# Hybrid convolution and RG-LRU layer: the last pair of lru tiles alone forked, with a PSUM tile for each of its four sums, and the remainders of four lru weights made on VectorE

## The chip, the cores and the metric

The kernel runs on one core of a Trainium2 chip. The metric is the device time of one execution in microseconds; smaller is better. The kernel before took 732.24, 734.92 and 737.24 us in three runs, with the median 734.92.

## The reference

One layer works on a sequence of 1024 tokens of 1024 channels, in float32. The normalised and modulated input goes through a wide projection, whose columns feed two groups side by side: a convolution group (gated depthwise convolution of 31 taps, layer norm over channels, swish, and the pointwise product `pw2`) and a recurrence group (RG-LRU). Both results are joined and go through the output projection, whose result is scaled by a gate and added to the input.

```
u = h @ w_in[l]
cv, cg, cs, lx, ls = jnp.split(u, [...], axis=-1)
...
v = jax.nn.silu(layernorm(v, cln_g[l], cln_b[l]))
v = v @ pw2_w[l] + pw2_b[l]
y_conv = v * jax.nn.silu(cs)
...
y_lru = hs * jax.nn.silu(ls)
y = jnp.concatenate([y_conv, y_lru], axis=-1) @ w_out[l]
x = x + (1.0 + gate[:, None, :]) * y
return rmsnorm(x, final_g)
```

The part of `w_out` that meets `y_lru` is what the change touches. It is called the lru product here.

## The kernel before, in words

**Number format.** TensorE works in a reduced float32 format. To keep accuracy, every operand is split into a high part and a remainder (`yh` and `yl`, `whi` and `wlo`), and each product is three matmuls: high by high, high by low, low by high. A weight comes from DRAM into `raw`; ScalarE casts it to `whi`; the remainder is `raw - whi`. There are two ways to make a remainder. One is a subtraction on VectorE (or, early in the kernel, GpSimd). The other, `remainder` at L540, lets ScalarE write `-whi` into `wlo` and then adds the weight itself from DRAM by an accumulating transfer that GpSimd issues. For the lru weights, the tuple `LRV` names those that take the VectorE way; all others take the transfer. The lru weights 0 to 7 bear the numbers 40 to 47 in tile names, so `wlo41` is the remainder of lru weight 1.

**Stages.** The layer runs in this order: modulation and first products; 40 column tiles of the input projection with the convolution and recurrence interleaved; the lru product, 8 output tiles of 128 x 1024 in four pairs p = 0 to 3; the pointwise product `pw2` in four pairs; the rest of `w_out`; and the final norm. While TensorE works on the lru product, VectorE and ScalarE finish the convolution and do the layer norm: sums of `c` and `cr` (`csum`, `mean`), squares (`lnsq`, collected in `lnss`), the spread of the result by TensorE (`lnbc`), and the splitting of the normalised tiles into the operands of `pw2` (`vha`, `vla`, `vhb`, `vlb`, `vhc`, `vlc` and the like).

**A pair of the lru product** (`lru_pair`, L1405) has two output tiles, each in two halves of 512 columns, and the inner dimension in eight blocks of 128. On four of the blocks the two-by-two product of halves is made with seven quarter products instead of eight, named 1, y, 2, z, 3, s and 4, over sums of operands (`yhs`, `yls` for the data, `lsh` and `lsl` for the weights). The other four blocks are multiplied plainly.

A quarter product appears in more than one output, so its value has to be used at several places while it grows. Pairs that are not forked (p = 0 and 1 before) do it outside PSUM: after each step, `use` (L1607) takes the partial value out of PSUM, scales it by the gate and adds it to the SBUF tile `acc`; the first step of each half is a ScalarE evacuation, later ones are VectorE operations on 512 columns. They use two PSUM tiles of two banks, `lp` and `lx`, and one of a single bank, `ly`. Forked pairs (`FORKP`, p = 2 and 3 before) do it inside PSUM: ScalarE copies the value after quarter 1 from `lx` to `lp`, and the quarter y from `lx` to a SBUF buffer `lk`; VectorE writes `lx + lk` into the second half of `lp` after quarter 2, and into the second half of `lx` after quarter 3; TensorE goes on adding in all four halves. At the end each tile is evacuated once, 1024 wide. All four sums live in the two tiles `lp` and `lx`; the class `Bank` lets the planner treat the two halves of such a tile as separate.

**What sets the order.** All engines' instructions are put in order at build time by a planner that simulates the engines (`order`, L241). Among the operations that are ready it takes the one with the lowest priority number; priorities are position numbers of the stages plus small offsets, and the pair p has position n = 40 + 2p. `FORKN` is the offset of the copies and sums of a forked pair, `FEVN` that of its evacuations, and `LSN` says how far back the start is that releases the loads of `lsh` and `lsl` (1: the quarter 2 of the pair before, 2: its first plain product). The engines then run these fixed orders, waiting on semaphores where an operand or a buffer isn't ready. Buffers are limited: PSUM has three tiles of two banks ("mm": `ps`, `lp`, `lx`) and two of one bank ("acc": `ly`); `raw`, `whi` and `wlo` have two slots each (lru weights 5 to 7 have large buffers in their place); and 47 large SBUF buffers are shared by nearly everything else, so that for instance `vla` or `vlc` takes a buffer that an `acc` tile held, and waits until the store of that tile (`accd`, an accumulating transfer that GpSimd issues) is through. GpSimd's queue in this part holds these stores and the remainders by transfer; SP's queue holds the loads.

Of the kernel before, what the change touches and what calls it, by code (L numbers as in the profile page):

```python
# [16 lines left out]
T = 1024  # L17
# [87 lines left out]
FINP = -0.5  # L105
BCLATE = False
BEHIND = 0
FORKP = (2, 3)
FORKN = -1.0
FEVAC = ("ACT", "ACT")  # L110
FEVN = 0.3
QT = {(0, c): ("HW", "X") for c in "y234"}
PLACED = ("big",)
MARGINS = 2.0
LSN = 1
LWBS = (5, 6, 7)
LWG = 0
TERMS = {**{("pw2_0", c): ("HW", "X") for c in "1z"}, **{(f"out_{p}", "1"): ("HX", "W") for p in (0, 1, 2, 3)}, **{(f"pw2_{p}", "1"): ("HX", "W") for p in (1, 2, 3)}}
# [38 lines left out]
class Buf:  # L157
    def __init__(self, pool, name, dtype, parts):
        self.pool, self.name, self.dtype, self.parts = pool, name, dtype, parts
        self.left, self.tile = 0, None  # L160
        self.read, self.written = {}, {}
        self.banks = None

    def __call__(self):
        return self.tile


class Bank:
    def __init__(self):
        self.read, self.written = {}, {}  # L170


class Op:
# [4 lines left out]
class Plan:  # L178
# [23 lines left out]
    def op(self, eng, cost, emit, prio, r=(), w=(), table=None, after=(), reserve=0,  # L202
           columns=0, lock=False, lag=0.0, moved=0.0, flight=FLIGHT):
        o = Op()
        o.lag, o.moved, o.flight = lag, moved, flight
        o.eng, o.cost, o.emit, o.prio, o.table = eng, cost, emit, prio, table
        o.succ, o.ready, o.seq, o.reserve = [], 0.0, len(self.ops), reserve
        o.columns = columns
        o.lock = not lag and eng == "POOL" or eng == "DVE" and lock
        r, w = list(self.keys(r)), list(self.keys(w))  # L210
        preds = set(after)
        for k in r:
            if k in self.writer:
# [17 lines left out]
        o.psum = [(b, any(k[0] is b for k in w)) for b in o.bufs if b.pool in ("mm", "acc") and not b.banks]  # L231
        o.psum += [(k[0].banks[k[1]], k in w) for k in dict.fromkeys(r + w) if isinstance(k[0], Buf) and k[0].banks]
        self.ops.append(o)
        return o

# [145 lines left out]
def hymba_layer(ctx: ExitStack, tc: tile.TileContext, xT, vecs, mod_w, w_first, w_in,  # L381
# [224 lines left out]
    def half(b, i):  # L606
        return part(b, i * H, i * H + H)
# [797 lines left out]
    def lru_pair(p, n, use, firsts, tiles):  # L1405
# [50 lines left out]
                ops.setdefault(c, o)  # L1456

        if p in FORKP:
            x.banks, p0.banks = [Bank(), Bank()], [Bank(), Bank()]

            def plain(s, ps, h):
                for k in rest:
                    mm_k(n + g, ps, s, yh, yl, k, FULL[h:h + 1], first=-1)

            def both(h, to):
                TT(n + FORKN, "DVE", half(to, 1), half(x, 0), half(kept, 0), ALU.add, H, r=[(x, 0), kept],
                   w=[(to, 1)])

            def out_of(i, ps):
                m = 2 * p + i  # L1470
                if FEVAC[i] == "ACT":
                    ACT(n + FEVN + i, tiles[i], ps, AF.Copy, scale=gate1[:, m:m + 1], r=[ps, ("gate1", m)],
                        w=[tiles[i]])
                else:
                    TS(n + FEVN + i, tiles[i], ps, gate1[:, m:m + 1], None, ALU.mult, r=[ps, ("gate1", m)],
                       w=[tiles[i]], n=T)
# [12 lines left out]
            g = 0.4  # L1489
            quarter("3", "S3", "T3", x, 0, False)  # L1490
            both(0, x)
            g = 0.5
            quarter("s", "S4", "B22", p0, 1, False)
            plain(s0, p0, 1)
            out_of(0, p0)
            g = 0.6
            quarter("4", "A22", "T4", x, 0, False)
            plain(s1, x, 0)
            g = 0.7
            plain(s1, x, 1)  # L1500
            out_of(1, x)
            return ops["1"], ops["3"]
        for c in LORDERS.get(p, LORDER):
            g += 0.12
# [368 lines left out]
```

## Time and profile before

| | us |
|---|---|
| three runs | 732.24, 734.92, 737.24 |
| profiled execution | 731.9 |
| its span on the core | 730.1 |
| TensorE busy in the span | 717.0 |
| VectorE busy | 619.3 |
| ScalarE busy | 481.0 |
| GpSimd busy | 170.3 |
| mean granted TensorE clock | 0.997 |

In the rows of the profile, PE is TensorE's matmuls and PEld its weight loads, DVE is VectorE, ACT is ScalarE, POOL is GpSimd, and SP issues loads. A row of the timeline gives the start, the duration, engine, line, operation, output and inputs by the program's names (numbers left out), shape and count, and in brackets how long the engine had been idle before it and what ended the idle time. A row of the windows gives, for a stretch of the span, its length and each engine's busy time. "L580" is the plain product's matmul, "L1448" that of a quarter, "L756" those of `pw2` and `w_out`; "L452" is any two-operand operation of VectorE, "L444" its scale-and-add, "L425" a copy or cast and "L433" any other operation of ScalarE, and "L457" a transfer issued by GpSimd.

### The profile page before, as it was taken

The numbers are of one execution on the slowest core, as the hardware profiler recorded it, in microseconds if no ns is written. First come the engines' busy times: TensorE is split into PE (matmuls) and PEld (weight loads), VectorE is DVE, ScalarE is ACT, GpSimd is POOL, SyncE is SP. The second block draws the span as 40 slices with busy tenths as digits, with TensorE's granted clock in tenths as the row PEclk, the third lists the DMA queues.
The fourth block names the chain that finished last, engine by engine and source line by source line (L and its number), as shares of the span: only waits on it lengthen the run. The fifth ranks groups of instructions, "written<-read, shape, count | busy, mean of one in ns | idle before, by whom it ended". The sixth has DMA issues, their size and how long they took to land.

```text
span 730.1 us, 9057 instructions
## 1 busy us (share of the span) xinstructions
PE 717.0 (98%) x3268; PEld 595.6 (82%) x3268; DVE 619.3 (85%) x851; ACT 481.0 (66%) x618; POOL 170.3 (23%) x172
## 2 busy tenths in 40 slices
PE   9999999999999999999999999999899999999996
PEld 8888888888888888888888888878778888888885
DVE  7999999899699898798499994989498966999647
ACT  7650789566698866947949869827488635746322
POOL 0046334354443320233221120100101101110003
PEclk9999999999999999999999999999999999999998
DMA  8946349949989996799898895876935855775006
GB/s 339 406 172 174 58 119 246 262 101 214 216 196 238 243 231 183 169 236 210 176 226 233 226 179 151 256 191 187 223 58 110 228 139 131 232 187 185 30 14 217
DMA packets 46779, 138.58 MB, mean 190 GB/s; under 512 B 5280, under 2 KB 16544, under 8 KB 46624
## 3 DMA queue, kind: packets, MB, share of 16 engines
q0 software_dynamic: 20016, 53.40, 40.9%
q1 hardware_dynamic: 25712, 83.71, 32.7%
q10 hardware_dynamic: 1008, 0.92, 0.4%
q8 instruction: 25, 0.41, 0.2%
q14 instruction: 18, 0.15, 0.1%
HBM read 79.63 MB, written 22.54 MB: 140 GB/s over the span
## 4 chain that ended last, share of the span: by engine, by line
PE 85%; DVE 6%; ACT 4%; issue 3%; DMA 1%; DVEq 0%; POOLq 0%; ACTq 0%
PE ps L580 43%; PE xout L756 6%; PE xpw L756 6%; PE first L889 5%; PE lx L1448 3%; PE ypw L756 3%; PE lp L580 2%; PE lx L580 2%; PE gate L1309 2%; DVE caccs L444 2%; PE y L726 2%; PE zpw L756 2%; PE zout L756 1%; DMA wlo<-in_w_out_dram 1%; PE lp L1448 1%
## 5 line engine op out<-in xcount | busy, mean ns | idle before, releaser
L580 PE MATMUL ps<-uh,whi 128*128 128x512 f32 x576 | 177.5, 389 | 0.0
L580 PE MATMUL ps<-uh,wlo 128*128 128x512 f32 x576 | 177.3, 389 | 0.0
L580 PE MATMUL ps<-ul,whi 128*128 128x512 f32 x576 | 177.3, 389 | 0.0
L580 PEld LDWEIGHTS ps<-ul,whi 128*128 128x128 f32 x576 | 108.1, 188 | 22.5
L580 PEld LDWEIGHTS ps<-uh,wlo 128*128 128x128 f32 x576 | 108.1, 188 | 22.4
L580 PEld LDWEIGHTS ps<-uh,whi 128*128 128x128 f32 x576 | 108.0, 188 | 22.4
L457 POOL DMA_DIRECT2D es<-cq x45 | 40.2, 899 | 134.2 <-ACT cq L433 85.5
L425 ACT CAST whi<-raw 128x1024 fp32r<-128x1024 f32 (+1 forms) x44 | 44.9, 1026 | 37.4 <-issue 22.3
L452 POOL TENSOR_TENSOR wlo<-raw,whi 128x1024 fp32r<-128x1024 f32 x16 | 40.6, 2547 | 87.4 <-ACT whi L425 87.1
L433 ACT ACT_TABLE_LOAD x44 | 56.5, 1283 | 1.5 <-PEq L1865 0.7
L444 DVE SCALAR_TENSOR_TENSOR cacc<-v,V,cacc 128x511 f32<-128x511 f32 (+14 forms) x75 | 55.6, 741 | 0.4
L444 DVE SCALAR_TENSOR_TENSOR caccs<-v,V,caccs 128x511 f32<-128x511 f32 (+6 forms) x70 | 51.9, 742 | 2.0 <-ACT caccs L433 1.0
L444 DVE SCALAR_TENSOR_TENSOR caccs<-c,wsum,caccs 128x511 f32<-128x511 f32 (+6 forms) x70 | 52.0, 743 | 1.0
L457 POOL DMA_DIRECT2D oo<-co x39 | 37.2, 996 | 45.5 <-ACT co L433 20.4
L433 ACT ACTIVATE cq<-v,V 128x511 f32<-128x511 f32 (+14 forms) x45 | 31.8, 707 | 4.5 <-DVE modw L444 4.5
L452 DVE TENSOR_TENSOR wlo<-raw,whi 128x1024 fp32r<-128x1024 f32 (+1 forms) x23 | 27.4, 1194 | 8.4 <-ACT whi L425 8.4
L444 DVE SCALAR_TENSOR_TENSOR modw<-modw,sc 128x1024 f32<-128x1024 f32 x23 | 31.4, 1369 | 0.2 <-DMA modw<-in_mod_w_dram 0.2
L444 DVE SCALAR_TENSOR_TENSOR xs<-ps,V,xs 128x1023 f32<-128x1023 f32 (+2 forms) x24 | 30.6, 1273 | 0.5 <-ACT xs L433 0.5
L433 ACT ACTIVATE cq<-c,wsum 128x512 f32<-128x512 f32 x42 | 29.7, 711 | 0.0
L433 ACT ACTIVATE co<-v,V 128x510 f32<-128x510 f32 (+12 forms) x39 | 26.6, 706 | 0.0
L433 ACT ACTIVATE finsq<-fin 128x512 f32<-128x512 f32 (+2 forms) x14 | 7.9, 570 | 27.4 <-DVE fin L444 14.4
L452 POOL TENSOR_TENSOR o<-fin,bc 128x256 f32<-128x256 f32 (+1 forms) x8 | 7.8, 999 | 68.0 <-ACT bc L425 62.3
(409 smaller groups left out, 1591.4 us busy)
## 6 DMA issues: line engine op xcount, KB each, us to landing
raw<-in_w_in_dram SPq DMA_DIRECT2D x36, 512.0 KB, 5.8
modw<-in_mod_w_dram SPq DMA_DIRECT2D x24, 512.0 KB, 8.3
scsd<-scs SPq DMA_DIRECT2D x8, 512.0 KB, 4.3
raw<-in_w_out_dram SPq DMA_DIRECT2D x8, 512.0 KB, 3.8
accd<-acc POOLq DMA_DIRECT2D x8, 512.0 KB, 6.6
rawpw<-in_pw_dram SPq DMA_DIRECT2D x8, 512.0 KB, 5.0
scsr<-scsd SPq DMA_DIRECT2D x8, 512.0 KB, 5.8
rawout<-in_w_out_dram SPq DMA_DIRECT2D x8, 512.0 KB, 3.3
```

Of the source, the lines that this page charges most:

```text
L425: act.copy(out(), in_())
L433: act.activation(out=out(), in_=in_(), func=func, **kw)
L444: dve.scalar_tensor_tensor(out=out(), in0=in0(), scalar=scalar, in1=in1(), op0=op0, op1=op1, accum_out=accum)
L452: lambda: e.tensor_tensor(out=out(), in0=a(), in1=b(), op=op), prio, r, w,
L457: return S.op("POOL", ISSUE, lambda: pool.dma_start(out(), a(), accum_op=ALU.add), prio, r, w, lag=RATE * n / T, after=after, flight=flight)
L580: pe.matmul(ps()[:, a - off:b - off], k3(lhs)()[:, at, :], rhs[k]()[:, a:b], start=(k == first and lhs is wh and rhs is xh and (a - off) % ...
L726: pe.matmul(to(), half(*lhs)()[:, j * P:j * P + P], half(*rhs)()[:, c0:c1], start=a == "S1" and j == 0 and t == 0, stop=j == KT // 2 - 1 a ...
L756: pe.matmul(half(ps, 0)(), half(*lhs)()[:, j * P:j * P + P], half(*rhs)(), start=start and at == 0 and i == 0, stop=at == len(order) - 1 a ...
L889: pe.matmul(ps()[:, a - off:b - off], fw_part(lhs, k, i * P, i * P + P)(), rhs()[:, a:b], start=k == 0 and lhs is wh and rhs is xh, stop=k ...
L1309: pe.matmul(ps()[:, c0:c1], lhs()[:, j, :], rhs()[:, c0:c1], start=st == 0, stop=st == 2)
L1448: pe.matmul(half(ps, h)(), lhs()[:, o:o + P], half(*rhs)(), start=begin and at == 0 and t == 0, stop=at == len(order) - 1 and t == len(ter ...
```

## The change

Five settings change. `FORKP` names pair 3 alone, so pair 2 takes the unforked way. `LRV` names the lru weights 1, 2, 4 and 5 where it named 3, 4 and 5: the remainders of 41 and 42 move to VectorE, and that of 43 moves to ScalarE and the transfer. `LSN` goes from 1 to 2, `FORKN` from -1.0 to -3.0 and `FEVN` from 0.3 to 0.1. `FEVD` replaces `FEVAC`: a forked pair is now evacuated half by half, three halves by ScalarE and the last one, (1, 1), by VectorE. `QRES` also gets another value, and is read nowhere in the program.

The code of the forked pair gives each of the four sums a PSUM tile: `lx` for the first half of the second output tile, `lw` (a "mm" tile of which one half is used) for its second half, and the one-bank tiles `lc` and `ld` for the two halves of the first. The copy after quarter 1 goes from `lx` to `lc`, quarter y is made in `lw` and copied to `lk`, and the two VectorE sums go to `ld` and `lw`. The class `Bank` and what used it are gone. The number of matmuls of a pair is the same.

```diff
-FORKP = (2, 3)
-FORKN = -1.0
-FEVAC = ("ACT", "ACT")
-FEVN = 0.3
+FORKP = (3,)
+FORKN = -3.0
+FEVD = ((1, 1),)
+FEVN = 0.1
-LSN = 1
+LSN = 2
-LRV = (3, 4, 5)
-QRES = 0
+LRV = (1, 2, 4, 5)
+QRES = 3
...
-            x.banks, p0.banks = [Bank(), Bank()], [Bank(), Bank()]
+            y0, y1, x1 = acc_tile(f"lc{p}"), acc_tile(f"ld{p}"), mm_tile(f"lw{p}")
...
-            def both(h, to):
-                TT(n + FORKN, "DVE", half(to, 1), half(x, 0), half(kept, 0), ALU.add, H, r=[(x, 0), kept],
-                   w=[(to, 1)])
+            def both(to):
+                TT(n + FORKN, "DVE", half(to, 0), half(x, 0), half(kept, 0), ALU.add, H, r=[(x, 0), kept],
+                   w=[(to, 0)])
...
-            def out_of(i, ps):
-                m = 2 * p + i
-                if FEVAC[i] == "ACT":
-                    ACT(n + FEVN + i, tiles[i], ps, AF.Copy, scale=gate1[:, m:m + 1], r=[ps, ("gate1", m)],
-                        w=[tiles[i]])
+            def out_of(i, h, ps):
+                m, to = 2 * p + i, half(tiles[i], h)
+                if (i, h) in FEVD:
+                    TS(n + FEVN + g, to, half(ps, 0), gate1[:, m:m + 1], None, ALU.mult, r=[(ps, 0), ("gate1", m)],
+                       w=[(tiles[i], h)], n=H)
                 else:
...
             quarter("1", "A11", "B11", x, 0, True)
-            ACT(n + FORKN, half(p0, 0), half(x, 0), "copy", H, r=[(x, 0)], w=[(p0, 0)])
+            ACT(n + FORKN, half(y0, 0), half(x, 0), "copy", H, r=[(x, 0)], w=[y0])
             g = 0.1
-            quarter("y", "S1", "T1", x, 1, True)
+            quarter("y", "S1", "T1", x1, 0, True)
             kept = big_buf(f"lk{p}")
-            ACT(n + FORKN, half(kept, 0), half(x, 1), "copy", H, r=[(x, 1)], w=[kept])
+            ACT(n + FORKN, half(kept, 0), half(x1, 0), "copy", H, r=[(x1, 0)], w=[kept])
             g = 0.2
             quarter("2", "S2", "T2", x, 0, False)
-            both(0, p0)
+            both(y1)
             g = 0.3
-            quarter("z", "A12", "B21", p0, 0, False)
-            plain(s0, p0, 0)
+            quarter("z", "A12", "B21", y0, 0, False)
+            plain(s0, y0, 0)
+            out_of(0, 0, y0)
...
```

Since the planner sets the order anew, the change also moves instructions on every engine. In the rows below a name ends in a serial number. The first place is VectorE at the start of the lru product, where the remainders `yl` of the recurrence's output are made. Before:

```order
L452 TENSOR_TENSOR yl4_3851<-sls4_2880,yh4_3804 128x1024
L452 TENSOR_TENSOR yls01_3861<-sls1_1636,yhs01_3849 128x1024
L452 TENSOR_TENSOR sls3_2386<-sls3_2386 128x512
L452 TENSOR_TENSOR yl5_3880<-sls5_3224,yh5_3824 128x1024
L452 TENSOR_TENSOR yl6_3893<-sls6_3414,yh6_3827 128x1024
L452 TENSOR_TENSOR yls11_3904<-sls3_2386,yhs11_3882 128x1024
L452 TENSOR_TENSOR yl7_3913<-sls7_3597,yh7_3837 128x1024
```

and now:

```order
L445 TENSOR_TENSOR yl4_3851<-sls4_2880,yh4_3804 128x1024
L445 TENSOR_TENSOR yls01_3861<-sls1_1636,yhs01_3849 128x1024
L445 TENSOR_TENSOR wlo41_3874<-raw41_3725,whi41_3859 128x768
L445 TENSOR_TENSOR sls3_2386<-sls3_2386 128x512
L445 TENSOR_TENSOR yl5_3887<-sls5_3224,yh5_3824 128x1024
L445 TENSOR_TENSOR yl6_3899<-sls6_3414,yh6_3827 128x1024
L445 TENSOR_TENSOR yls11_3909<-sls3_2386,yhs11_3891 128x1024
L445 TENSOR_TENSOR yl7_3919<-sls7_3597,yh7_3837 128x1024
```

The remainder of weight 41 stands ahead of the last four remainders of y; the order of the others is the same.

The second place is GpSimd's queue from the start of the lru product to the second store of pair 2 (`accd5`). Before:

```order
L457 DMA wlo40_3780<-in_w_out_dram 128x1024
L457 DMA wlo41_3875<-in_w_out_dram 128x768
L457 DMA wlo42_3954<-in_w_out_dram 128x1024
L457 DMA accd0_120<-acc0_3891 128x1024
L457 DMA accd1_121<-acc1_3972 128x1024
L457 DMA accd2_122<-acc2_4076 128x1024
L457 DMA wlo46_4166<-in_w_out_dram 128x1024
L457 DMA accd3_123<-acc3_4133 128x1024
L457 DMA wlo47_4200<-in_w_out_dram 128x768
L457 DMA accd4_124<-acc4_4301 128x1024
L457 DMA accd5_125<-acc5_4352 128x1024
```

and now:

```order
L450 DMA wlo40_3780<-in_w_out_dram 128x1024
L450 DMA accd0_120<-acc0_3885 128x1024
L450 DMA accd1_121<-acc1_3968 128x1024
L450 DMA wlo43_4031<-in_w_out_dram 128x768
L450 DMA accd2_122<-acc2_4097 128x1024
L450 DMA wlo46_4156<-in_w_out_dram 128x1024
L450 DMA wlo47_4179<-in_w_out_dram 128x768
L450 DMA accd3_123<-acc3_4149 128x1024
L450 DMA accd4_124<-acc4_4239 128x1024
L450 DMA accd5_125<-acc5_4292 128x1024
```

Two transfers for remainders, 41 and 42, are gone from the front, and one, 43, stands behind the store `accd1` of pair 0; the transfers for 46 and 47 stand ahead of `accd3`.

The third place is VectorE in the layer norm, which lies beside pair 2. `lnss` collects the squares, `rs` is the reciprocal of the deviation, and the rows with `lnbc` scale the tiles by it. Before:

```order
L452 TENSOR_TENSOR lnss_4051<-lnss_4051,lnsq6_4183 128x1024
L452 TENSOR_TENSOR lp2_4193<-lx2_4179,lk2_4205 128x512
L452 TENSOR_TENSOR lnss_4051<-lnss_4051,lnsq7_4211 128x1024
L820 RECIPROCAL rs-1_0_4241<-sd-1_0_4239 128x8
L452 TENSOR_TENSOR cr0_3839<-cr0_3839,lnbc_4227 128x1024
L452 TENSOR_TENSOR c1_942<-c1_942,lnbc_4227 128x1024
L452 TENSOR_TENSOR lx2_4179<-lx2_4179,lk2_4205 128x512
L452 TENSOR_TENSOR cr2_3853<-cr2_3853,lnbc_4227 128x1024
L452 TENSOR_TENSOR c3_1401<-c3_1401,lnbc_4227 128x1024
```

and now:

```order
L445 TENSOR_TENSOR lnss_4065<-lnss_4065,lnsq5_4169 128x1024
L445 TENSOR_TENSOR lnss_4065<-lnss_4065,lnsq6_4195 128x1024
L445 TENSOR_TENSOR lnss_4065<-lnss_4065,lnsq7_4205 128x1024
L813 RECIPROCAL rs-1_0_4246<-sd-1_0_4244 128x8
L437 SCALAR_TENSOR_TENSOR acc4_4239<-lp2_4151,gate1_95,acc4_4239 128x512
L445 TENSOR_TENSOR cr0_3839<-cr0_3839,lnbc_4230 128x1024
L445 TENSOR_TENSOR c1_942<-c1_942,lnbc_4230 128x1024
L437 SCALAR_TENSOR_TENSOR acc4_4239<-lx2_4223,gate1_95,acc4_4239 128x512
L445 TENSOR_TENSOR cr2_3853<-cr2_3853,lnbc_4230 128x1024
L445 TENSOR_TENSOR c3_1401<-c3_1401,lnbc_4230 128x1024
L445 TENSOR_TENSOR cr4_3872<-cr4_3872,lnbc_4230 128x1024
L437 SCALAR_TENSOR_TENSOR acc5_4292<-lx2_4223,gate1_95,acc5_4292 128x512
```

The sum `lp2<-lx2,lk2` ahead of the last `lnss` is gone with the second one, and four scale-and-adds of `acc4` and `acc5` stand behind the collecting, among the rows with `lnbc`.

More of the change, by code (lines that the diff above doesn't have):

```diff
@@ L161, in __init__ @@
         self.read, self.written = {}, {}
-        self.banks = None
     def __call__(self):
         return self.tile
-class Bank:
-    def __init__(self):
-        self.read, self.written = {}, {}
 class Op:
@@ L230, in op @@
             b.left += 1
-        o.psum = [(b, any(k[0] is b for k in w)) for b in o.bufs if b.pool in ("mm", "acc") and not b.banks]
-        o.psum += [(k[0].banks[k[1]], k in w) for k in dict.fromkeys(r + w) if isinstance(k[0], Buf) and k[0].banks]
+        o.psum = [(b, any(k[0] is b for k in w)) for b in o.bufs if b.pool in ("mm", "acc")]
         self.ops.append(o)
@@ L1458, in lru_pair @@
         if p in FORKP:
-            x.banks, p0.banks = [Bank(), Bank()], [Bank(), Bank()]
+            y0, y1, x1 = acc_tile(f"lc{p}"), acc_tile(f"ld{p}"), mm_tile(f"lw{p}")
             def plain(s, ps, h):
                 for k in rest:
-                    mm_k(n + g, ps, s, yh, yl, k, FULL[h:h + 1], first=-1)
-            def both(h, to):
-                TT(n + FORKN, "DVE", half(to, 1), half(x, 0), half(kept, 0), ALU.add, H, r=[(x, 0), kept],
-                   w=[(to, 1)])
-            def out_of(i, ps):
-                m = 2 * p + i
-                if FEVAC[i] == "ACT":
-                    ACT(n + FEVN + i, tiles[i], ps, AF.Copy, scale=gate1[:, m:m + 1], r=[ps, ("gate1", m)],
-                        w=[tiles[i]])
-                else:
-                    TS(n + FEVN + i, tiles[i], ps, gate1[:, m:m + 1], None, ALU.mult, r=[ps, ("gate1", m)],
-                       w=[tiles[i]], n=T)
+                    mm_k(n + g, ps, s, yh, yl, k, FULL[h:h + 1], off=h * H, first=-1)
@@ new lines, in both @@
+            def both(to):
[6 more added lines that the diff above has]
+                       w=[(tiles[i], h)], n=H)
+                else:
+                    ACT(n + FEVN + g, to, half(ps, 0), AF.Copy, H, scale=gate1[:, m:m + 1],
+                        r=[(ps, 0), ("gate1", m)], w=[(tiles[i], h)])
@@ L1494, in lru_pair @@
-            plain(s0, p0, 1)
-            out_of(0, p0)
+            quarter("s", "S4", "B22", y1, 0, False)
+            plain(s0, y1, 1)
+            out_of(0, 1, y1)
             g = 0.6
@@ L1498, in lru_pair @@
             plain(s1, x, 0)
+            out_of(1, 0, x)
             g = 0.7
-            plain(s1, x, 1)
-            out_of(1, x)
+            plain(s1, x1, 1)
+            out_of(1, 1, x1)
             return ops["1"], ops["3"]
```

3 lines of the change are left out of this document (1 added, 2 removed).

## The prediction, made before the changed kernel was run

> **What bounds the kernel now.** I read the page's first part, then the chain that ended last, then a table of windows by stage.
>
> ```profile
> PE 717.0 (98%) x3268; PEld 595.6 (82%) x3268; DVE 619.3 (85%) x851; ACT 481.0 (66%) x618; POOL 170.3 (23%) x172
> PE 85%; DVE 6%; ACT 4%; issue 3%; DMA 1%; DVEq 0%; POOLq 0%; ACTq 0%
> core 0: us, PE busy (x) PEld busy (x) DVE busy (x) ACT busy (x) POOL busy (x), PEclk, DMA share, GB/s
> 386.00:470.00 84.00, 84.00 (x372) 69.57 (x371) 71.41 (x78) 71.00 (x78) 13.09 (x15) 1.00 0.83 211
> 470.00:483.00 13.00, 11.52 (x51) 9.20 (x49) 12.96 (x17) 7.97 (x11) 1.34 (x2) 1.00 0.85 256
> 565.00:640.00 75.00, 75.00 (x331) 61.77 (x330) 58.13 (x82) 43.78 (x57) 9.60 (x11) 1.00 0.68 185
> 640.00:700.00 60.00, 60.00 (x265) 49.31 (x264) 49.88 (x74) 27.78 (x41) 1.73 (x2) 1.00 0.40 117
> 470.03:563.30 93.27, 87.99 (x397) 71.36 (x396) 76.32 (x90) 59.03 (x73) 11.42 (x13) 1.00 0.65 153
> ```
>
> The reader should see that PE never rests in the stages before 470 and from 565 to 700, that the clock is 1.00 throughout, and that it loses time between 470.03 (first lru matmul) and 563.30 (first pw2 matmul), where all of the change lies. In that stretch the PE timeline (start us, duration us, idle before and its releaser) shows six stalls, and the two runs of layer-norm matmuls (lnbc):
>
> ```profile
> 470.03 0.39 PE L1448 MATMUL lx<-yh,whi 128*128 128x512 f32 x1
> 481.14 0.39 PE L580 MATMUL ly<-yl,whi 128*128 128x512 f32 x1
> 483.03 0.50 PE L580 MATMUL ly<-yh,wlo 128*128 128x512 f32 x1 [1.50 <-DMA wlo<-in_w_out_dram]
> 516.50 0.50 PE L1448 MATMUL lx<-yhs,lsh 128*128 128x512 f32 x1 [0.71 <-ACT lp L425]
> 518.83 0.50 PE L1448 MATMUL lx<-yhs,lsh 128*128 128x512 f32 x1 [0.68 <-ACT lk L425]
> 521.35 0.50 PE L1448 MATMUL lp<-yh,whi 128*128 128x512 f32 x1 [0.86 <-DVE lp L452]
> 523.54 1.84 PE L803 MATMUL lnbc<-ones,lnss 128*128 128x1 f32 x16
> 525.24 0.47 PE L580 MATMUL lp<-yh,whi 128*128 128x512 f32 x1
> 543.64 0.50 PE L1448 MATMUL lx<-yhs,lsh 128*128 128x512 f32 x1 [0.66 <-ACT lp L425]
> 548.21 0.50 PE L580 MATMUL lp<-yh,whi 128*128 128x512 f32 x1 [0.86 <-DVE lp L452]
> 563.30 0.39 PE L756 MATMUL xpw<-vha,whipw 128*128 128x512 f32 x1
> 563.53 0.39 PE L756 MATMUL xpw<-vha,wlopw 128*128 128x512 f32 x1
> ```
>
> One matmul follows another at 0.23 us (563.30 to 563.53; over nine rows of that product 0.227). The 397 of the window row are 364 of 512 columns, 32 small lnbc ones and the tail of one that began before. So the stretch needs 364 x 0.227 = 82.5 for the matmuls and twice 1.70 for lnbc (523.54 to 525.24, and the like for the second): 85.9 of 93.27. **7.3 us is the most the change can take off here**: the listed idle is 1.50 + 0.71 + 0.68 + 0.86 + 0.66 + 0.86 = 5.3, and the rest is the slower start of a matmul after a stall (from start to start 481.14 to 483.03 is 1.89, so 1.66 over the pitch; the six together 6.2) and slightly slack rows behind it.
>
> **The change, part by part.** *LRV.* Weight 41's remainder comes from DVE in place of ACT and a POOL transfer, so the 1.66 us stall at 483.03 goes. Its price is one subtraction of 768 columns:
>
> ```profile
> 494.47 0.95 DVE L452 TENSOR_TENSOR wlo<-raw,whi 128x768 fp32r<-128x768 f32 x1
> 474.59 1.21 DVE L452 TENSOR_TENSOR yls<-sls,yhs 128x1024 fp32r<-128x1024 f32 x1
> 475.72 1.21 DVE L452 TENSOR_TENSOR yl<-sls,yh 128x1024 fp32r<-128x1024 f32 x1
> ```
>
> It stands ahead of the last lows of y on DVE, the busiest engine there (12.96 of 13.00). The rows behind move by 0.87: yl of tile 7 from 476.9 to 477.8. Since the changed order puts more of the lx and ly products first, its first use is the 38th matmul of the stretch (470.03 + 37 x 0.227 = 478.4), so 0.5 is spare and I cost it nothing; without that cover it is at most 0.87. Weight 42's subtraction (one of 1024 columns, 1.13 of DVE time by the last two starts) stands between two additions out of PSUM; acc0<-lx then ends near 483.9, and PE wants its bank at 484.3; the next such use has 0.3. I put 0.2 for these.
>
> Weight 43 goes the other way: ACT makes the negative, POOL's accumulating transfer adds the weight.
>
> ```profile
> 493.20 0.83 ACT L425 CAST whi<-raw 128x768 fp32r<-128x768 f32 x1
> 495.03 0.89 POOL L457 DMA_DIRECT2D accd<-acc  x1 [4.64 <-ACT acc L433]
> DMA to landing us min/median/max: 9.9/9.9/9.9
> DMA to landing us min/median/max: 10.7/10.7/10.7
> DMA to landing us min/median/max: 5.3/5.3/5.3
> ```
>
> The landings are those of the tile wlo, of weights 41 and 47 (768 columns) and 42 (1024). The buffer for whi43 is free when PE is through weight 41, 93 matmuls in: 470.03 + 21.1, with 0.3 for the hand-over 491.4. Cast and negative (0.83 each) end near 493.6 with ACT's queue, the transfer starts behind the store of acc1 near 493.8, and lands between 499.1 and 504.5. PE needs it 153 matmuls in, at 504.7: a margin of 0.2 to 5.6. I take 9.9 as nearest in size, so no stall, and 0.3 for the thin margin. [...]
>
> *Pair 2 not forked.* Three stalls go: 0.71 + 0.68 + 0.86 of idle, each with 0.16 of slow start behind it (1.66 - 1.50), 2.7. Added are four DVE additions out of PSUM and four ACT halves, against two DVE additions, two ACT copies and two wide ACT evacuations. What was queued behind the forked sum on DVE is the layer norm:
>
> ```profile
> 480.61 0.74 DVE L444 SCALAR_TENSOR_TENSOR acc<-lp,gate,acc 128x512 f32<-128x512 f32 x1
> 481.27 0.73 DVE L444 SCALAR_TENSOR_TENSOR acc<-lx,gate,acc 128x512 f32<-128x512 f32 x1
> 520.60 0.70 DVE L452 TENSOR_TENSOR lp<-lx,lk 128x512 f32<-128x512 f32 x1 [3.95 <-PE lp L1448]
> 521.20 1.22 DVE L452 TENSOR_TENSOR lnss<-lnss,lnsq 128x1024 f32<-128x1024 f32 x1
> 528.70 1.22 DVE L452 TENSOR_TENSOR cr<-cr,lnbc 128x1024 f32<-128x1024 f32 x1 [2.77 <-PE lnbc L809]
> 538.95 0.68 DVE L452 TENSOR_TENSOR vu<-cr 128x512 f32<-128x512 f32 x1
> 539.55 0.68 DVE L452 TENSOR_TENSOR vt<-c,cr 128x512 f32<-128x512 f32 x1
> 547.45 0.70 DVE L452 TENSOR_TENSOR lp<-lx,lk 128x512 f32<-128x512 f32 x1 [1.67 <-PE lp L1448]
> 570.13 1.22 DVE L452 TENSOR_TENSOR vlb<-c,vhb 128x1024 fp32r<-128x1024 f32 x1
> ```
>
> DVE sits 3.95 us before that sum with the last lnss behind it. Without it lnss is done near 518.2 in place of 522.4, PE reaches lnbc at 519.2 and DVE gets lnbc's result at 524.3 in place of 528.7: 4.4 earlier. That matters, for the next late thing is DVE itself: vlb of 570.13 ends at 571.35 and PE takes it at 571.40. From 528.70 to 571.35 are 42.65 us, waits among them (the longest 1.67). In the changed order the same span of DVE work is 17 operations of 1024 columns at 1.13, 31 of 512 at 0.60 (538.95 to 539.55), three additions out of PSUM at 0.66 (480.61 to 481.27) and one evacuation at 0.60: 40.4 to 41 us without a pause, so it ends at 524.3 + 41 = 565.3. PE, six matmuls later in its new order (41 past the first of pw2), wants it at 556.0 + 41 x 0.227 = 565.3. No slack is left: whatever DVE waits in between shows at the end, and I put 0.4 for it.
>
> *Pair 3 forked into four PSUM tiles.* The sum for the second half has a tile of its own, so its stall at 548.21 (0.86 + 0.16) goes (the sum ready at 541, wanted at 543.8). The first copy, from ACT, is still just in time: ready 538.3, wanted 538.3, against 0.66 + 0.16 lost before. I put 0.3. Its fourth evacuation is a DVE operation of 0.60, counted above.
>
> *LSN and the rest.* The loads of lsh and lsl are released earlier and stand ahead of raw 45 on SP; they were no releaser of any stall, so nothing. FORKN sets the order that I walked; QRES is read nowhere.
>
> Sum: 7.3 - (0.2 + 0.3 + 0.4 + 0.3) = **6.1**. After the first pw2 products nothing is reordered and PE is full until 700, so it stays to the end. The profiled execution took 731.9 (span 730.1 and 1.8 around it), and would take 725.8; on the median of the three runs, 734.92, that is **728.8**. The three runs span 732.24 to 737.24, so about 1% is what a measurement of this kernel tells from no change, and 1% of the median is 7.35: the whole bound.
>
> **The rivals.** *Part of the gain only.* A late landing leaves a stall at weight 43, and DVE waits for the stores of acc4 and acc5, whose buffers vla and vlc take over. Of the tile accd, the eight stores, and the one of 536.35:
>
> ```profile
> L457 POOL DMA_DIRECT2D accd<-acc x8: 865/875/893, 489.5 to 565.2; - x8
> DMA to landing us min/median/max: 5.2/6.6/9.7
> DMA to landing us min/median/max: 5.4/5.4/5.4
> ```
>
> The store of acc5 starts near 537.6 and vlc wants its buffer at 543.8, so 6.2 us of landing are free; at 8.5 DVE loses 2.3 and PE with it, at 9.7 it loses 3.5. That gives a gain of 2.5 to 4 us: 731 to 732.5. For it speaks that half of those eight stores took more than 6.6; against it that the one nearest in time took 5.4.
>
> *The gain is hidden.* If DVE's chain from lnbc to vlb is some 4 to 6 us longer than I add up (every added operation also passes the queue, and evacuations wait for PE), PE meets it at 571 as now: 733 to 735. DVE's idle shares (76.3 busy of 93.3 in the stretch) speak against that.
>
> *Slower.* One mechanism: weight 43's transfer now stands on PE's path. It starts at 493.8 and has 10.9 us; it eats the whole gain when it lands after 493.8 + 10.9 + 6.1 = 510.8, so from a landing of 17 us on, and at 20 us the kernel ends 3 us later than before, near 738. [...] Against a long delay stand the three landings above under a DVE that was busy 12.96 of 13.00 us at the first: 9.9 there, and 10.7 at 517.6, when DVE sat idle until 520.60. No landing on this queue in the stretch is near 17.
>
> **Chances.** Forecast (gain 5 to 7.3) 0.60; part of it 0.20; hidden 0.10; slower 0.10. Range: the forecast alone, 727.6 to 730 with the measurement's spread 726 to 731; with the part gain and half of the hidden case 725.5 to 735.5. Faster by over 1% needs the full bound or a lucky median: 0.22, all from the forecast. Slower by over 1% needs a landing past 24 us or a DVE chain longer by 13, and is given 0.10, the whole of that rival. Within 1%: 0.68.
>
> **What would show it.** No releaser DMA wlo at ly of weight 41; no ACT lp or lk stall in pair 2; lnss ending near 518; lnbc's product on DVE near 524.3; first pw2 matmul near 557; vlb near 565.3. Wrong: a stall of PE at weight 43 with releaser DMA wlo, or DVE waiting behind accd between 540 and 548, or PE waiting for vlb.

## The result, and the profile after

The changed kernel is faster: 725.74 us in the median of six runs (724.5 to 725.9) against 732.62 for the kernel before in six runs (731.64 to 737.24). The ratio is 0.989 with a 95% interval of 0.9863 to 0.9917, so the change is clear of noise. The profiled execution took 725.0 us with a span of 723.2, which is 6.9 less than before in both.

The prediction had the way and the place right. It said 6.1 us and held "within 1%" the likeliest; the gain is 6.9 us, 0.94% by the medians and 1.1% by the ratio of 0.989.

The page, the windows and the waits of TensorE after the change, beside those quoted in the prediction:

```profile
PE 715.4 (99%) x3268; PEld 596.5 (82%) x3268; DVE 622.6 (86%) x855; ACT 478.6 (66%) x618; POOL 169.5 (23%) x171
PE 99%; DVE 0%; DVEq 0%; issue 0%; ACT 0%
470.00:483.00 13.00, 13.00 (x59) 10.76 (x58) 13.00 (x16) 6.54 (x9) 0.00 (x0) 1.00 0.60 225
483.00:520.00 37.00, 37.00 (x167) 30.58 (x165) 33.19 (x35) 20.64 (x26) 6.12 (x7) 1.00 0.78 191
545.00:565.00 20.00, 20.00 (x90) 16.57 (x89) 20.00 (x27) 16.43 (x22) 4.39 (x5) 1.00 0.84 195
470.47:556.74 86.27, 86.27 (x398) 71.74 (x396) 78.51 (x93) 57.39 (x73) 10.52 (x12) 1.00 0.67 161
PE token_stats L839 <- DVE ones L495: 1.1, 1, 1.1
PE finbc L802 <- DVE rs65.7_0_5839 L813: 0.9, 1, 0.9
```

The chain that ended last is now TensorE by 99%, where it was 85% with VectorE, ScalarE and a transfer in between. All six stalls are gone; the two waits that are left lie at the start and the end of the kernel and were there before. The stretch from the first lru matmul to the first pw2 matmul takes 86.27 us in place of 93.27, with TensorE busy in all of it. It is the cleanest measure here, since the first lru matmul starts anywhere from 469.85 to 471.07 in the profiles of this case: here at 470.47, before at 470.03. The experiments below are compared by this stretch, by what lies behind it, and by the medians. What lies behind it took 166.80 us before and 166.46 now. Where a run is said to end above the changed kernel, its median is set against 725.74; the median of the kernel before was 732.24 to 732.74 in the several sets of runs.

How close the next limits came shows on the other engines. Their timelines (start us, duration us) and the landing of weight 43:

```profile
515.21 3.89 DVE L445 TENSOR_TENSOR lnss<-lnss,lnsq 128x1024 f32<-128x1024 f32 x3
524.87 1.22 DVE L445 TENSOR_TENSOR cr<-cr,lnbc 128x1024 f32<-128x1024 f32 x1 [1.03 <-PE lnbc L802]
538.31 0.58 ACT L418 COPY lc<-lx 128x512 f32<-128x512 f32 x1
539.01 0.43 PE L1441 MATMUL lx<-yhs,lsh 128*128 128x512 f32 x1
564.41 1.23 DVE L445 TENSOR_TENSOR vlb<-c,vhb 128x1024 fp32r<-128x1024 f32 x1
566.03 0.39 PE L749 MATMUL zpw<-vlb,whipw 128*128 128x512 f32 x1
494.61 0.87 POOL L450 DMA_DIRECT2D wlo<-in_w_out_dram  x1
DMA to landing us min/median/max: 7.3/7.3/7.3
505.19 0.39 PE L573 MATMUL ly<-yh,wlo 128*128 128x512 f32 x1
```

The last lnss ends at 519.1 (predicted 518.2) and lnbc's product starts at 524.87 (524.3). vlb of tile 3 ends at 565.64 (565.3), and TensorE takes it at 566.03: about 0.4 us to spare after 41 us of VectorE work without a pause. Weight 43's transfer starts at 494.6 (493.8) and lands at 501.9, 3.3 us ahead of the matmul at 505.19. The copy into lc ends at 538.89, and the matmul behind it starts at 539.01. These times are 0.3 to 0.9 us behind the predicted ones, and 0.44 of that is the later start of the whole stretch.

### The profile page after: what moved, and what is told of

Same layout as the page of the kernel before. It is cut to its first block, busy times and chain, and to the rows that moved or that the text cites. A ratio compares the mean times of both kernels' runs of the same rounds, so it can differ in the third digit from the quotient of the medians.

```text
span 723.2 us, 9061 instructions
## 1 busy us (share of the span) xinstructions
PE 715.4 (99%) x3268; PEld 596.5 (82%) x3268; DVE 622.6 (86%) x855; ACT 478.6 (66%) x618; POOL 169.5 (23%) x171
## 4 chain that ended last, share of the span: by engine, by line
PE 99%; DVE 0%; DVEq 0%; issue 0%; ACT 0%
PE ps L573 54%; PE xout L749 6%; PE xpw L749 6%; PE first L882 5%; PE lx L1441 3%; PE ypw L749 3%; PE gate L1302 3%; PE lp L573 2%; PE y L719 2%; PE zout L749 2%; PE zpw L749 2%; PE lx L573 2%; PE lp L1441 1%; PE yout L749 1%; PE ly L573 1%; PE late L882 1%
## 5 line engine op out<-in xcount | busy, mean ns | idle before, releaser
L437 DVE SCALAR_TENSOR_TENSOR modw<-modw,sc 128x1024 f32<-128x1024 f32 x23 | 29.6, 1290 | 0.0
L450 POOL DMA_DIRECT2D accd<-acc x8 | 7.0, 878 | 71.3 <-DVE acc L437 53.0
```

What stands on the lines that cost most here:

```text
L437: dve.scalar_tensor_tensor(out=out(), in0=in0(), scalar=scalar, in1=in1(), op0=op0, op1=op1, accum_out=accum)
L450: return S.op("POOL", ISSUE, lambda: pool.dma_start(out(), a(), accum_op=ALU.add), prio, r, w, lag=RATE * n / T, after=after, flight=flight)
```

## The experiments

Two readings of the gain were set against each other. **Stall by stall:** TensorE alone limits the stretch, and each of its stalls is worth its own length. **One chain:** the way through the layer norm on VectorE sets the end, and only what shortens it pays. A setting of this kernel never changes one thing alone, since the planner orders everything behind it anew; so each run was read by the stalls that its trace shows, not by its time only.

### Parts of the change by themselves

Three runs put one or two settings on the kernel before, and the fourth takes the un-forking of pair 2 out of the changed kernel.

```diff
# a1_lrv, on the kernel before
-LRV = (3, 4, 5)
+LRV = (1, 2, 4, 5)
# a2_fork, on the kernel before
-FORKP = (2, 3)
+FORKP = (3,)
# a3_both, on the kernel before: both of these
# a4_fork23, on the changed kernel
-FORKP = (3,)
+FORKP = (2, 3)
```

> The kernel before with LRV = (1, 2, 4, 5) alone. Theory (stall by stall: TensorE is the only limit of the lru stretch, and each of its stalls is worth its own length): the 1.7 us stall at weight 41 goes and the five stalls of the forked pairs stay; 1.7 us less than before, a stretch from the first lru to the first pw2 matmul of about 91.6 us. Rival (one chain: the way through the layer norm on VectorE sets the end, so only what lets lnss end earlier pays): PE waits elsewhere for what it gained, less than 0.5 us off.

> The kernel before with FORKP = (3,) alone, pair 3 still in two tiles. Stall by stall: the three stalls of pair 2 go (2.7 us), the one at weight 41 (1.7) and two of pair 3 (1.8) stay; 2.7 us less than before, stretch about 90.5 us. One chain: nearly the whole gain of the changed kernel, 6 us or more.

> The kernel before with LRV = (1, 2, 4, 5) and FORKP = (3,), pair 3 still in two tiles. Stall by stall: 4.4 to 5.4 us less than before; pair 3's two stalls (0.8 and 1.0) are the only ones left, so 1.5 to 2 us above the changed kernel. One chain: equal to the changed kernel within 0.5 us, since pair 3 lies behind the layer norm.

> The changed kernel with FORKP = (2, 3), both pairs in four PSUM tiles. Stall by stall: the waits for the two sums stay away, those for the two copies by ScalarE come back in pair 2 (0.7 each with 0.16 of slow start), 1 to 1.7 us above the changed kernel. One chain: the sum of pair 2 stands behind the last lnss in VectorE's order here, so no layer norm is held up; equal to the changed kernel within 0.5 us.

| run | median us | ratio to before (95%) | stretch us | stalls of TensorE, us of idle |
|---|---|---|---|---|
| before | 732.5 | | 93.27 | 1.50; 0.71, 0.68, 0.86; 0.66, 0.86 |
| LRV alone | 731.91 | 0.999 (0.9981 to 0.9998) | 92.52 | 0.74 new; 0.71, 0.68, 0.86; 0.66, 0.86 |
| FORKP alone | 729.33 | 0.9955 (0.9942 to 0.9969) | 90.46 | 1.64; 0.66, 0.86 |
| LRV and FORKP | 730.37 | 0.9964 (0.9951 to 0.9976) | 89.35 | 0.66, 0.68, 0.86; 1.50 new |
| changed, pair 2 forked too | 726.72 | 0.9916 (0.9904 to 0.9928) | 87.67 | 0.27, 0.62, both new |

LRV alone: the stall at weight 41 is gone, but TensorE now waits for a VectorE addition in pair 1. The first row is the kernel before, the other two this run:

```profile
508.44 0.74 DVE L444 SCALAR_TENSOR_TENSOR acc<-lx,gate,acc 128x512 f32<-128x512 f32 x1
508.38 0.74 DVE L444 SCALAR_TENSOR_TENSOR acc<-lx,gate,acc 128x512 f32<-128x512 f32 x1
509.17 0.50 PE L1448 MATMUL lx<-yhs,whi 128*128 128x512 f32 x1 [0.74 <-DVE acc L444]
```

The addition comes no later than before; TensorE comes earlier, since it ran this matmul at 509.50 before and would reach it near 508.3 now. The stretch is 0.75 us shorter: 1.66 saved, 0.74 and a slow start of 0.16 given back. Stall by stall had said 1.7 less and missed; as its rival had it, TensorE waits elsewhere for part of what it gained, though not in the layer norm. FORKP alone brought what stall by stall had said, 2.8 us of stretch with the stalls of pair 2 gone and the others where they were; one chain had said 6 or more, and falls here. With both, the gain in the stretch is 3.9 and by the medians only 2.1 (4.4 to 5.4 had been expected): the new order holds three stalls in pair 3 instead of two, and TensorE waits 1.50 us behind the stretch, in the first pw2 pair, for a ScalarE evacuation. Neither reading foresaw that one. In the last run pair 2 is forked again, and neither a copy nor a sum holds TensorE up. Stall by stall had expected the copies to; the two small waits that came are for pair 1, one for a ScalarE evacuation (0.27) and one for a VectorE addition (0.62). That the run ended 1.0 us above the changed kernel, inside the 1 to 1.7 that were expected, is luck: the waits are others.

Why the copies no longer stall shows in two rows of the kernel before and three of the changed one:

```profile
515.88 0.57 ACT L425 COPY lp<-lx 128x512 f32<-128x512 f32 x1 [0.92 <-PE lx L1448]
516.50 0.50 PE L1448 MATMUL lx<-yhs,lsh 128*128 128x512 f32 x1 [0.71 <-ACT lp L425]
537.65 0.39 PE L1441 MATMUL lw<-yhs,lsh 128*128 128x512 f32 x1
538.31 0.58 ACT L418 COPY lc<-lx 128x512 f32<-128x512 f32 x1
539.01 0.43 PE L1441 MATMUL lx<-yhs,lsh 128*128 128x512 f32 x1
```

Before, the matmul at 516.50 is the first of quarter y, which goes to the second half of `lx`; it waited until the copy had read the first half. ScalarE had been idle for 0.92 us and began the copy as soon as quarter 1 was through, so an earlier place in its order (the new FORKN) could not have brought it forward. Now quarter y goes to `lw` and runs from 537.65 on, and the copy is done beside it.

### The tiles alone, the remainders as before, and LSN

```diff
# d1_tiles, on the changed kernel: its code and settings for a forked pair stay, the rest is as before
-FORKP = (3,)
+FORKP = (2, 3)
-LSN = 2
+LSN = 1
-LRV = (1, 2, 4, 5)
+LRV = (3, 4, 5)
# b1_lrvold, on the changed kernel
-LRV = (1, 2, 4, 5)
+LRV = (3, 4, 5)
# b2_lsn1, on the changed kernel
-LSN = 2
+LSN = 1
# d2_lsn2, on the kernel before
-LSN = 1
+LSN = 2
```

> The changed kernel with FORKP = (2, 3), LRV = (3, 4, 5) and LSN = 1: of the change only the four PSUM tiles of a forked pair (with the halved evacuation) are left. Stall by stall: the five stalls of the forked pairs go (4.6 us), the one at weight 41 stays (1.7): 4.6 us less than the kernel before, if no new wait comes. Rival (the four tiles matter only for pair 3, the gain of pair 2 is from not forking it): 1.8 us less.

> The changed kernel with LRV = (3, 4, 5) as before. Stall by stall: the wait of TensorE for weight 41's transfer comes back with 1.5 to 1.7 us and nothing else does, since pairs 2 and 3 keep the changed form: 1.7 us above the changed kernel. Rival (the remainders on VectorE cost as much as they save, as the run with LRV alone hints): within 0.5 us of the changed kernel.

> The changed kernel with LSN = 1. As predicted, the earlier loads of lsh and lsl are worth nothing: within 0.5 us of the changed kernel. Rival: LSN moves the order of everything in pairs 2 and 3, as in the run with LRV and FORKP, where a wait of 1.5 us for a ScalarE evacuation appeared in the first pw2 pair; then 1.5 to 2.5 us above the changed kernel.

> The kernel before with LSN = 2 alone. As predicted, earlier loads of lsh and lsl are worth nothing by themselves, since no stall has them as releaser: within 0.5 us of before, the six stalls as before. Rival: through the order of VectorE it is worth 1.5 us or more, as its absence cost in the changed kernel.

| run | median us | ratio to before (95%) | stretch us | stalls of TensorE, us of idle |
|---|---|---|---|---|
| four tiles alone | 730.84 | 0.997 (0.9956 to 0.9983) | 89.00 | 1.22; 0.34 new; 1.54 new behind the stretch |
| changed, LRV as before | 727.01 | 0.9927 (0.9912 to 0.9942) | 88.13 | 1.60 |
| changed, LSN = 1 | 727.39 | 0.9932 (0.9917 to 0.9947) | 86.30 | 1.53 new behind the stretch |
| before, LSN = 2 | 731.8 | 0.9979 (0.9967 to 0.9992) | 91.92 | 1.26; 0.71, 0.68; 0.71, 0.86 |

The four tiles take the five stalls of the forked pairs away and bring 4.27 us of stretch, with one small new stall of 0.34 for a sum of pair 3 (`ld`). But TensorE waits 1.54 us behind the stretch, what lies there takes 2.0 us more than before (168.83 against 166.80), and the medians show a gain of only 1.9. That this comes near the 1.8 of the rival is luck: the rival had the stalls of pair 2 staying, and they are gone. This run keeps FORKN, FEVN and the evacuation by halves as well, and what these are worth was not separated. With LRV as before the one stall at weight 41 is back and the stretch is 1.86 us longer, and no other wait is listed: in the finished order LRV is worth its whole stall.

LSN was costed at nothing, and is not nothing. With LSN = 1 the changed kernel has the same stretch (86.30), but waits in the first pw2 pair and ends 1.65 us above by the medians, as the rival had said. The timelines of that run, ScalarE and then TensorE:

```profile
567.52 2.25 ACT L418 CAST h34pw<-rawpw 128x1024 fp32r<-128x1024 f32 x2 [1.19 <-DVE rawpw L445]
569.67 0.68 ACT L426 ACTIVATE yc<-ypw,V 128x512 f32<-128x512 f32 x1
570.41 0.50 PE L749 MATMUL ypw<-vhb,h34pw 128*128 128x512 f32 x1 [1.53 <-ACT yc L426]
```

Two casts of the next pair's weights stand ahead of the evacuation of `ypw` here, and the first of them waits for VectorE. In the changed kernel the evacuation stands ahead of both, and runs before them:

```profile
568.04 0.69 ACT L426 ACTIVATE yc<-ypw,V 128x512 f32<-128x512 f32 x1 [1.27 <-PE ypw L749]
569.22 1.05 ACT L418 CAST h34pw<-rawpw 128x1024 fp32r<-128x1024 f32 x1 [0.48 <-DVE rawpw L445]
```

The same wait, 1.50 to 1.54, stands in all three runs with LSN = 1 beside another new setting (LRV and FORKP, four tiles alone, and this one), though not in those with FORKP or LRV alone. On the kernel before, LSN = 2 takes 1.35 us off the stretch and 0.9 off the median, less than the rival's 1.5 and more than the 0.5 that was expected. There the last lnss is ahead of the forked sum in VectorE's order, and the stall of 0.86 for that sum in pair 2 is gone:

```profile
517.71 1.23 DVE L452 TENSOR_TENSOR lnss<-lnss,lnsq 128x1024 f32<-128x1024 f32 x1 [0.81 <-ACT lnsq L433]
520.84 0.70 DVE L452 TENSOR_TENSOR lp<-lx,lk 128x512 f32<-128x512 f32 x1 [1.91 <-PE lp L1448]
```

In both cases its worth is the order that the planner makes of it, not the earlier load: no stall in any trace names lsh or lsl as its releaser.

### How near the other limits are

The first of these makes three subtractions twice on VectorE; the next two hold the transfer of weight 43 back by GpSimd work ahead of it; the last moves the remainder of weight 43 to VectorE as well. In the first three the order of the instructions is that of the changed kernel.

```diff
# c1_dve
-                    SUB(p, "DVE", lo, src, hi, T, [src, hi], [lo])
+                    SUB(p, "DVE", lo, src, hi, T, [src, hi], [lo],
+                        again=2 if lo.name in ("vlb0", "vlb1", "vlb2") else 1)
# c3_late43 (again = 3) and c4_later43 (again = 6), for weight 43
-        ACT(prio, lo, lambda: hi().bitcast(F32), AF.Copy, n, scale=-1.0, ...)
+        ACT(prio, lo, lambda: hi().bitcast(F32), AF.Copy, n, scale=-1.0 / 2 ** again, ...)
...
+            for _ in range(again):
+                pool.tensor_tensor(out=out(), in0=out().bitcast(F32), in1=out().bitcast(F32), op=ALU.add)
             pool.dma_start(out(), a(), accum_op=ALU.add)
# b4_lrvall
-LRV = (1, 2, 4, 5)
+LRV = (1, 2, 3, 4, 5)
```

> The changed kernel with three subtractions of the pw2 operands (vlb of tiles 0 to 2, 1024 columns, 1.13 us each) made twice on VectorE, with the order unchanged. If VectorE had no slack left between lnbc and vlb of tile 3, as predicted (the changed trace shows 0.35 us), TensorE waits there about 3.0 us and the kernel takes 3 us more than the changed one. Rival (VectorE is hidden behind TensorE): within 0.5 us.

> The changed kernel with three additions on GpSimd (768 columns, an estimated 1.9 us each from the 2.55 us of 1024 columns) ahead of the transfer of weight 43; the first operand is scaled down so that the values stay the same. In the changed trace the transfer starts at 494.6, lands 7.3 later, and TensorE wants it at 505.2, a margin of 3.3 us: 5.7 us more leave a stall of 2.4 us with DMA wlo as its releaser, and the kernel takes about 2.4 us more than the changed one (0.4 to 5.8 with landings of 5.3 to 10.7). Rival: the margin is larger than the trace says, and the time stays within 0.5 us.

> As the run with three additions ahead of the transfer of weight 43, but with six (5.75 us for three were measured, so 11.5). The transfer starts near 506.5 and lands 4.7 to 10 us later, at 511 to 517; TensorE wants it at 506.5, so it waits 5 to 10 us with DMA wlo as its releaser, and the kernel takes 5.5 to 10.5 us more than the changed one. Rival: pair 1 has other work to give and the time rises by less than 2 us.

> The changed kernel with LRV = (1, 2, 3, 4, 5): the remainder of weight 43 on VectorE too (0.95 us). Since that transfer landed 3.3 us ahead of its use, nothing is to be had: within 0.5 us of the changed kernel, if the planner's order brings no new wait. Rival: VectorE, which is without slack from the layer norm on, passes its 0.9 us on to TensorE.

| run | median us | ratio to before (95%) | stretch us | stalls of TensorE, us of idle |
|---|---|---|---|---|
| 3.4 us more on VectorE | 729.36 | 0.9959 (0.9944 to 0.9973) | 86.31 | 2.27 and 0.63 for vlb |
| transfer held back by 3 additions | 726.22 | 0.9917 (0.99 to 0.9933) | 87.24 | 0.66 for csl |
| by 6 additions | 734.04 | 1.0006 (0.9992 to 1.0019) | 95.60 | 0.66 for csl, 5.31 for wlo |
| weight 43 on VectorE too | 732.25 | 0.9983 (0.9972 to 0.9994) | 87.40 | 0.74; 1.44 and 1.45 behind the stretch |

**VectorE is the next limit, with almost nothing in hand.** Of the 3.4 us that were added, 2.9 came out as waits of TensorE for vlb, first for that of tile 2 and then for that of tile 3. The two rows below them are windows of 2 us (length, busy time and count of TensorE, its weight loads, VectorE, ScalarE and GpSimd, the granted clock in the third column from the end):

```profile
564.79 0.50 PE L750 MATMUL zpw<-vlb,whipw 128*128 128x512 f32 x1 [2.27 <-DVE vlb L445]
570.08 0.50 PE L750 MATMUL zpw<-vlb,whipw 128*128 128x512 f32 x1 [0.63 <-DVE vlb L445]
562.00:564.00 2.00, 0.52 (x3) 0.10 (x1) 1.97 (x3) 1.57 (x2) 0.66 (x1) 1.00 1.15 322
564.00:566.00 2.00, 1.21 (x5) 1.02 (x6) 2.00 (x3) 0.69 (x3) 0.00 (x0) 1.00 0.88 158
```

The rest is near the slack of 0.4. By the medians it is 3.6 us slower than the changed kernel.

**The transfer of weight 43 has its 3 us.** Held back by three additions it started at 500.8 and landed 4.7 later, at 505.5, sooner after its start than the 7.3 of the changed kernel; TensorE wanted it at 506.51, itself delayed, and did not wait for it. The 2.4 us that were expected did not come, and this run leaves the price of a late landing open. What it did show is a slower subtraction on VectorE while GpSimd ran its additions:

```profile
494.60 5.75 POOL L451 TENSOR_TENSOR wlo<-wlo 128x768 fp32r<-128x768 f32 x3
495.33 2.15 DVE L445 TENSOR_TENSOR csl<-csum,csh 128x1024 fp32r<-128x1024 f32 x1 [1.68 <-ACT csh L418]
498.31 1.22 DVE L445 TENSOR_TENSOR cr<-cr,mean 128x1024 f32<-128x1024 f32 x1 [0.82 <-PE mean L1548]
```

In the changed kernel that subtraction takes 1.23. The one at 498.31, also beside the additions, takes 1.22 as ever; its operand `mean` lies in PSUM. With six additions the transfer starts near 505.5 (an estimate: its issue takes 0.89 us with three additions, and GpSimd is busy for 0.40 of the window from 506 to 508) and lands near 511.5, where the matmul that waited for it starts; the wait predicted for a late landing is there. The matmul, and windows of 2 us behind it:

```profile
511.52 0.79 PE L577 MATMUL ly<-yh,wlo 128*128 128x512 f32 x1 [5.31 <-DMA wlo<-in_w_out_dram]
510.00:512.00 2.00, 0.48 (x1) 0.48 (x2) 1.56 (x2) 0.00 (x0) 0.60 (x1) 0.64 1.02 209
512.00:514.00 2.00, 2.00 (x6) 1.52 (x6) 0.00 (x0) 0.00 (x0) 0.00 (x0) 0.50 1.05 190
514.00:516.00 2.00, 2.00 (x7) 1.51 (x6) 0.00 (x0) 0.00 (x0) 0.00 (x0) 0.50 0.11 21
516.00:518.00 2.00, 2.00 (x7) 1.59 (x6) 0.00 (x0) 1.81 (x3) 0.00 (x0) 0.65 0.00 0
```

This wait of 5.31 us cost more than itself: the clock is at 0.50 in the windows from 512 to 516, matmuls follow each other at 0.43 in place of 0.23 up to 517.23, and the stretch is 9.33 us longer than in the changed kernel. Of that, 1.0 came already with three additions, so about 3 are on top of the wait. The whole gain is gone, at a wait of 5.3 us; the rival, which counted the wait alone, had put that at 6.1.

**One subtraction more undoes nearly all of it.** Weight 43 on VectorE was to change nothing, or 0.9 us by the rival. It costs 6.5 us by the medians, and only 1.1 of it lies in the stretch. Behind it TensorE waits for vha, whose chain comes through VectorE, and for vla of VectorE itself:

```profile
570.87 0.50 PE L749 MATMUL ypw<-vha,h34pw 128*128 128x512 f32 x1 [1.44 <-ACT vha L418]
572.82 0.74 PE L749 MATMUL ypw<-vla,h34pw 128*128 128x512 f32 x1 [1.45 <-DVE vla L445]
569.00:571.00 2.00, 0.56 (x3) 0.13 (x1) 2.00 (x5) 1.75 (x3) 0.30 (x1) 1.00 0.95 147
571.00:573.00 2.00, 0.55 (x2) 0.24 (x3) 2.00 (x4) 0.76 (x1) 0.00 (x0) 0.98 1.05 192
573.00:575.00 2.00, 2.00 (x5) 1.58 (x6) 2.00 (x3) 1.60 (x2) 0.00 (x0) 0.50 0.85 237
575.00:577.00 2.00, 2.00 (x7) 1.55 (x6) 2.00 (x4) 1.50 (x4) 0.00 (x0) 0.67 0.14 57
```

VectorE is busy in each of these windows. Behind these two waits of 1.44 and 1.45 us the clock was 0.50 as well (573 to 575). How much of the two waits is the 0.9 us more on VectorE, and how much the new order, was not separated.

## Why the prediction was right, and where it was not

**The bound** was right. TensorE was said to need 85.9 us for the stretch; it took 86.27, and 7.0 of the 7.3 us that could go went. As it said, nothing of this was lost behind the stretch.

**The stall at weight 41** went, and came back with 1.60 us when LRV alone was put back. That the subtraction costs nothing held in the whole change. With LRV alone a stall of 0.74 came, not at yl, where the prediction had looked for the price, but at an addition of pair 1; so it is free in the changed order, not everywhere.

**Pair 2** lost its three stalls, and un-forking it alone is worth 2.8 (predicted 2.7). That lnss ends earlier and lnbc with it held as well: 528.70 became 524.87. But un-forking isn't the only way to that: pair 2 forked into four PSUM tiles has no wait for a copy or a sum either, in both runs that had it.

**VectorE as the next limit without slack** was right to a few tenths: 0.4 us were left, and of 3.4 more, 2.9 reached TensorE. The rival of a hidden gain had no ground: the sum of VectorE's chain, 41 us, held with 40.8. Nor did the part gain come: VectorE had no wait between 524.87 and 565.64, so none for a store, and the store of acc5, which started at 537.68, landed 5.4 us later, within the 6.2 that were free.

**LSN at nothing** was wrong. Without it the changed kernel is 1.65 us slower by the medians, by an order of ScalarE in the first pw2 pair that no trace of before shows. Since the whole new order was laid down ahead of the run, this didn't bend the total; as a statement on the part it fails.

**The rival of the slower end** (the transfer of weight 43) had the right mechanism and a price somewhat too low, but the landing stayed at 7.3, and at 4.7 and 6.0 in the two runs that held it back; none came near the 17 us that it needed.

**The step that failed** is the size of the four allowances in the sum: 0.2 for banks freed late in pair 0, 0.3 for weight 43, 0.4 for VectorE's chain and 0.3 for the first copy of pair 3, 1.2 in all. The trace after lists no wait at any of them. Of the 0.37 by which the stretch is over the need, 0.19 lies in the first matmuls behind the two lnbc products, which the prediction had at the common pitch of 0.227:

```profile
521.39 0.49 PE L1441 MATMUL lp<-yh,whi 128*128 128x512 f32 x1
521.72 0.40 PE L1441 MATMUL lp<-yl,whi 128*128 128x512 f32 x1
524.58 0.47 PE L1441 MATMUL ly<-yhs,lsh 128*128 128x512 f32 x1
524.90 0.39 PE L1441 MATMUL ly<-yls,lsh 128*128 128x512 f32 x1
```

At the four places only the matmul behind the copy into lc, 0.12 us after the copy's end, shows a trace of a loss: 0.03. So the four terms measured 0.03 together in place of 1.2. Two of them had been worked out with time to spare, two as exactly even (538.3 against 538.3, 565.3 against 565.3), and each was charged as if it were a loss. That is the difference between 6.1 and 6.9 us: without them the sum is 7.3, against 7.0 in the stretch and 6.9 over the kernel. The allowances also set the likeliest outcome: 6.1 lies below the 7.35 that stood for 1%, and the measured ratio of 0.989 lies a little past it. Two other things were off. The median of three runs, 734.92, was 2.3 us above that of six, so the forecast of 728.8 carried 2.3 us of it on top of 0.8 from the allowances, the 3.1 by which it missed. And the 1%, read from the spread of three runs, was too coarse a bar: the comparison of six and six has an interval of 0.27% to either side, so "within 1%" was no fitting name for a forecast gain of 0.8%.

## What to carry to other kernels

Where one engine is busy nearly all the time and its waits can be listed one by one, the stretch between two of its instructions, minus what its work needs, bounds a change well, and the instruction order with the measured durations tells which waits go. A place where the walk finds TensorE not kept waiting should be charged nothing in the sum and go into the range alone. A setting of a planner is never one edit: its worth (LSN, weight 43) can lie wholly in an order somewhere else, so read the new order at the end of the stage too, and expect the parts not to add up.

## What the runs showed of the hardware

**In two runs the granted clock was 0.50 behind waits of TensorE.** With a wait of 5.31 us it was 0.50 in the windows from 512 to 516, and matmuls followed each other at 0.43 us in place of 0.23 up to 517.23, 5.7 us from the end of the wait. It was 0.50 as well behind two waits of 1.44 and 1.45 us (573 to 575), when TensorE had been busy for 1.11 of 4 us (569 to 573), and 1.00 beside and behind waits of 2.27 and 0.63 that ended 5 us apart, with TensorE busy for 1.73 of 4 us (562 to 566). So the longest single wait does not tell the last two cases apart, and the busy share of those 4 us does; where the bound lies, these runs do not show.

**In the rows compared here, VectorE took longer beside a GpSimd addition or subtraction when both its operands lay in SBUF, and not when one lay in PSUM.** The subtraction of csl, with both in SBUF, took 2.15 us in both runs with GpSimd additions beside it and 1.23 without them; that of `mean`, which lies in PSUM, took 1.22 beside them. Three subtractions of GpSimd in the changed kernel, each with rows of VectorE beside it (`ps` and `cacc` lie in PSUM, the other operands in SBUF), read alike:

```profile
112.56 2.40 POOL L445 TENSOR_TENSOR wlo<-raw,whi 128x1024 fp32r<-128x1024 f32 x1 [2.86 <-ACT whi L418]
113.46 2.58 DVE L445 TENSOR_TENSOR xsl<-xs,xsh 128x1024 fp32r<-128x1024 f32 x1 [0.24 <-ACT xsh L418]
136.84 2.39 POOL L445 TENSOR_TENSOR wlo<-raw,whi 128x1024 fp32r<-128x1024 f32 x1 [4.06 <-ACT whi L418]
137.29 3.02 DVE L445 TENSOR_TENSOR sls<-sls,r 128x1024 f32<-128x1024 f32 x1
147.72 2.41 POOL L445 TENSOR_TENSOR wlo<-raw,whi 128x1024 fp32r<-128x1024 f32 x1 [5.33 <-ACT whi L418]
147.06 1.23 DVE L445 TENSOR_TENSOR v<-ps,sig 128x1024 f32<-128x1024 f32 x1 [3.62 <-PE ps L573]
148.20 0.68 DVE L445 TENSOR_TENSOR c<-c,cacc 128x512 f32<-128x512 f32 x1
```

Without GpSimd beside them xsl takes 1.22, sls 1.21 to 1.23, v 1.22 to 1.23, and c with cacc 0.68 to 0.69. What in the chip makes the difference, the runs do not show.
